# An MLP up-projection as seven block products, its gated product kept in DRAM, and a down-projection that stays in PSUM

## The chip, the core and the metric

The kernel runs on one core of a Trainium2 chip. The metric is device time in microseconds (us). Before the change three runs took 2066.19, 2067.78 and 2071.95 us; the median, 2067.78 us, is the time before.

## What is computed

One transformer block on 1024 tokens of width 1024, all in float32. The change concerns its last part, the residual after the token mixer and the gated MLP with a three-tap convolution over the tokens:

```python
x = x + gt1 * _rmsnorm(y, norm_w[l, 1])                 # y: output of the token mixer, times w_o
h = _rmsnorm(x, norm_w[l, 2]) * (1.0 + sc2) + sh2
hu = _dwconv(h @ w_up, conv_w, FFN_CONV // 2) + conv_b  # w_up: 1024 x 5632
a, b = jnp.split(hu, 2, axis=-1)
y = (jax.nn.silu(a) * b) @ w_down                       # w_down: 2816 x 1024
x = x + gt2 * _rmsnorm(y, norm_w[l, 3])
```

## The kernel before

Every float32 product is made of three float32r products. `split` copies a tile to a rounded high part on ScalarE (L166) and takes the rest as the low part on VectorE or GpSimd (L169). `mm3` (L171) then issues high by high, high by low and low by high into one PSUM group, so a product over K blocks of 128 is 3K matmuls of 128x128 by 128x512. All matmuls have line L128, all transposes L131, which are helpers. Where `T.kept` is set, TensorE follows the program's order; elsewhere a scheduler orders each engine, and each engine works off its own queue in order.

The end of the kernel, from about 1232 us on, goes so:

- `wo_tile(t)` (L1408): for 128 tokens, two PSUM groups `y` of 24 matmuls, with block k = 7 of both halves last. Behind them a chain over ScalarE, VectorE and GpSimd: Square with a running sum (L1423), mean and power -0.5 (L1424 to L1426), scaling (L1429), residual (L1430), store to `x_d`, and the next norm (L1432 to L1435).
- `h2_half` (L1437): 128x128 transposes of four normed token tiles (`x1T`), modulation and split into `h2`, the transposed MLP input, for 512 tokens.
- `up_mm(f)` (L1465): 48 matmuls into a two-bank PSUM tile `hu` for one block f of 128 of the 5632 columns: two token halves, 8 blocks of k, 3 products. The weights `wur` come by DMA 512 KB at a time and are split into `wuh` and `wul`. 44 such blocks make 2112 matmuls.
- `up(f)` (L1504): the convolution as one ScalarE pass (L1508) and two VectorE passes (L1509, L1510). `pair(f)` (L1515): Silu (L1517) of block f, times block 22 + f (L1519), split into `gh` and `gl`.
- `down(c)` (L1542): for two f, 16 groups `yp` of 6 matmuls, each added by VectorE to a running sum `yac` in SBUF (L1551). `last_down` (L1553) takes the last four f, with the final norm and the output behind each token tile. In all 22 x 16 x 3 = 1056 matmuls.

The loop at L1578 to L1584 is four pairs, then in turn `down(c)` and two pairs, then `last_down`. So TensorE alternates between 192 matmuls of up and 96 of down, which have PSUM tiles of their own (2 two-bank tiles for up, 4 banks for down).

Of the kernel before, what the change touches and what calls it, by code (L numbers as in the profile page):

```python
# [32 lines left out]
def prep(inp):  # L33
# [45 lines left out]
    # constants of the shapes  # L79
# [15 lines left out]
class InOrder:  # L95
    """an engine whose instructions, those given here, stay in the order in which they are written"""
# [16 lines left out]
class Tensor:  # L113
    """the tensor engine's queue: kept in the order of the program while `kept`, with a rough clock in us"""
# [19 lines left out]
def build(nc, tc, I, out, dbg=None, stop=None):  # L134
# [87 lines left out]
    with ExitStack() as es:  # L222
# [71 lines left out]
        # token-major columns (beta, alpha, cq, ckv, kr): the first ones along with h  # L294
# [169 lines left out]
    # The tensor engine's queue: chains of dependent steps, each yielding the time until its next one  # L464
    # can start (and what has to be done before), and projections that fill the time between.
# [23 lines left out]
    def filling(convs, gates, w):  # L489
        """projections in turn, the weights of one loaded ahead of the other's use; w: those of the first"""  # L490
# [162 lines left out]
    def tail(h, c):  # L653
        """norm of the sum of both directions"""
# [35 lines left out]
    def head(h):  # L690
        """the norms, the products of k and q, and the rest of the chains of a head"""
# [72 lines left out]
        # token-major k, and v times each direction's beta  # L764
# [62 lines left out]
    def ada_steps():  # L827
        """the other four blocks of the modulation, in pieces to be laid between other work"""
# [35 lines left out]
    def z_steps(ob, h, z):  # L864
        """z of head h, times the normed output of its scans"""
# [102 lines left out]
    def c_norm(t, pl, jpl):  # L968
        """128 tokens of cq and ckv, each divided by its root mean square"""
# [429 lines left out]

    wuE = ExitStack()  # L1400
    wup = pool(wuE, "wup")
    x1E = ExitStack()
    x1p = pool(x1E, "x1p", side="right")
    x1 = [None] * KT
    h2 = [None, None]
    tp = pool(x1E, "so", side="right")

    def wo_tile(t):  # L1408
# [4 lines left out]
        x1[t] = x1p.tile([P, D], F32, tag="x1", name="x1", bufs=6)  # L1413
        pss = [ps_mm.tile([P, 512], F32, tag="mm", name="y") for _ in range(2)]
        for ks in (range(KT - 1), (KT - 1,)):
            for hf in range(2):
                sl = slice(hf * 512, hf * 512 + 512)
                for k in ks:
                    mm3(pss[hf], mg[hf_][0][k][:, c_], mg[hf_][1][k][:, c_], wo[k][0][:, sl], wo[k][1][:, sl], k == 0, k == KT - 1)
        junk = tp.tile([P, D], F32, tag="yj", name="yj")  # L1420
# [16 lines left out]
    def h2_half(hf, pl, tag):  # L1437
        """transposed, modulated and split, one block of columns at a step"""
        h2[hf] = btiles("h2")
        for k in range(KT):  # L1440
            pt = pl.tile([P, 512], F32, tag=tag, name="x1T")
            for j in range(4):
                T.transpose(pt[:, j * P : (j + 1) * P], x1[hf * 4 + j][:, k * P : (k + 1) * P], ident)
            f = tp.tile([P, 512], F32, tag="hf", name="hf2", bufs=2)
            if k % 2 == 0:
                A.activation(f, pt, AF.Identity, bias=sh2[:, k : k + 1], scale=sm2[:, k : k + 1])
            else:
                V.tensor_scalar(f, pt, sm2[:, k : k + 1], sh2[:, k : k + 1], op0=ALU.mult, op1=ALU.add)
            split(h2[hf][0][k], h2[hf][1][k], f)
            yield  # L1450

    for t in range(6):
        wo_tile(t)
    drain(h2_half(0, ps_dn, "dn"))
    wo_tile(6)
    wo_tile(7)
    psE.close()

# [1 line left out]
    psE = ExitStack()  # L1460
    ps_u = pool(psE, "ps_u", 2, space=PSUM)
    ps_y = pool(psE, "ps_y", 4, space=PSUM)
    NF = DFF // P

    def up_mm(f):  # L1465
        wh, wl = w_split(wup, I["w_up"][f], [P, KT, P], "wu", parts=2)
        ps = ps_u.tile([P, S], F32, tag="u", name="hu")

        def mms():
            for hf in range(2):  # L1470
                for k in range(KT):
                    mm3(ps[:, hf * 512 : hf * 512 + 512], wh[:, k, :], wl[:, k, :], h2[hf][0][k], h2[hf][1][k], k == 0, k == KT - 1)
                    yield

        return ps, mms()

    ups_ = {f: up_mm(f) for f in (0, NF)}
    T.kept = True
    (_, ua), (_, ub), tr = *ups_.values(), h2_half(1, ps_y, "y")
    steps = lambda it, n: [next(it) for _ in range(n)]  # L1480
    steps(ua, KT)
    steps(ub, 3)
    steps(tr, 3)
    steps(ub, KT - 3)
    for k in range(KT):
        steps(tr, int(k < KT - 3))
        steps(ua, 1)
        steps(ub, int(k > 2))
    drain(tr)
    T.kept = False  # L1490
    x1E.close()
    kvE.close()
    ffE = ExitStack()
    ff = pool(ffE, "ff")
    yac = [ff.tile([P, D], F32, tag=f"yac{t}", name=f"yac{t}") for t in range(KT)]
    with ExitStack() as es:
        tg = pool(es, "sg", side="right")
        tp = pool(es, "sf", side="right")
        fcw = tp.tile([P, 44, 3], F32, tag="fcw", name="fcw")
        SY.dma_start(fcw, I["f_conv"])  # L1500
        fcb = tp.tile([P, 44], F32, tag="fcb", name="fcb")
        SY.dma_start(fcb, I["f_cb"])
# [12 lines left out]
        def pair(f):  # L1515
            a = up(f)
            A.activation(a, a, AF.Silu)  # L1517
            b = up(NF + f)
            V.tensor_tensor(a, a, b, op=ALU.mult)  # L1519
            gh = tg.tile([P, S], F32R, tag="gh", name="gh", bufs=4)  # L1520
            gl = tg.tile([P, S], F32R, tag="gl", name="gl", bufs=4)
            split(gh, gl, a)
            gs[f] = (gh, gl)

        def load_down(f, hi, lo):
            raw = tg.tile([P, D], F32, tag="wdr", name="wdr", bufs=1)
# [26 lines left out]
        def last_down(fs):  # L1553
# [3 lines left out]
            for t in range(KT):  # L1557
# [12 lines left out]
                for hf in range(2):  # L1570
                    sl = slice(hf * 512, hf * 512 + 512)
                    V.scalar_tensor_tensor(xt[:, sl], yac[t][:, sl], s2[:, 0:1], xt[:, sl], op0=ALU.mult, op1=ALU.add)  # L1572
                    if t == KT - 1:
                        A.dma_start(out[t * P : (t + 1) * P, sl], xt[:, sl])
# [29 lines left out]
```

## Time and profile before

| | |
|---|---|
| median of 3 runs (lowest, highest) | 2067.78 us (2066.19, 2071.95) |
| profiled execution, first to last instruction (span) | 2064.6 us |
| TensorE (PE) busy | 2006.3 us, 97% |
| VectorE (DVE) / ScalarE (ACT) / GpSimd (POOL) busy | 58% / 37% / 16% |
| mean granted TensorE clock | 0.994 |

The profile comes from one execution, for which no time is listed beside its span; the span is 3.2 us under the median and 1.6 us under the lowest run. A busy share is an average over the whole kernel. What a stage can gain or lose is read from that stage, in its windows and in the chain of waits that ended last.

### The profile page before, as it was taken

To read this page: it belongs to the slowest core of one execution; us is meant where nothing else is said; L and a number is where in the kernel's file an instruction comes from. 1 tells how busy PE (TensorE), PEld (TensorE's weight loads), DVE (VectorE), ACT (ScalarE), POOL (GpSimd) and SP (SyncE) were. 2 spreads that over 40 slices of the span, in tenths; PEclk is the share of its full clock that TensorE was granted. 3 is DMA by queue.
4 is the path that set the end of the run, shared out by engine and by line. 5 is a ranking of instruction groups with operands and counts; after the bars stand their busy time and mean duration, and the time that the engine had idled before them with its cause. 6 is when DMAs were issued, how large, how long until landed. Compare 5 with 4: busy or idle time off the path is not lost. (4 is left out here: it accounts for less than half of the span.)

```text
span 2064.6 us, 27272 instructions
## 1 busy us (share of the span) xinstructions
PE 2006.3 (97%) x10846; PEld 1653.6 (80%) x10846; DVE 1204.4 (58%) x2032; ACT 769.1 (37%) x1314; POOL 320.1 (16%) x291
## 2 busy tenths in 40 slices
PE   7999999999999998899999999999999999999998
PEld 5978887888888797778777778878888888888886
DVE  7367867576666568674677654553435444445437
ACT  6464543353353222353545432443222222222222
POOL 4321131141041110233000031110100001000101
PEclk9999999999999999999999999999999999999999
DMA  8321121131021175454101163221111112111113
GB/s 291 112 72 62 43 72 57 47 113 62 32 99 66 44 262 193 149 158 151 53 11 32 41 200 106 73 82 41 52 52 51 42 42 62 41 51 41 51 47 137
DMA packets 68178, 175.09 MB, mean 85 GB/s; under 512 B 10257, under 2 KB 17745, under 8 KB 68050
## 3 DMA queue, kind: packets, MB, share of 16 engines
q1 hardware_dynamic: 54658, 143.13, 21.9%
q10 hardware_dynamic: 11088, 21.83, 2.8%
q0 software_dynamic: 2304, 8.39, 1.0%
q8 instruction: 85, 1.39, 0.3%
q14 instruction: 43, 0.35, 0.1%
HBM read 143.07 MB, written 30.24 MB: 84 GB/s over the span
## 5 line engine op out<-in xcount | busy, mean ns | idle before, releaser
L128 PE MATMUL hu<-h,wuh 128*128 128x512 f32 x1408 | 434.2, 390 | 1.6 <-DVE cv L1510 1.6
L128 PEld LDWEIGHTS hu<-h,wuh 128*128 128x128 f32 x1408 | 263.8, 188 | 56.6 <-ACT cv L1508 2.0
L128 PE MATMUL pj<-hhi,wth 128*128 128x512 f32 x704 | 294.1, 418 | 8.1 <-ACT vN L906 6.6
L128 PE MATMUL pj<-hhi,wtl 128*128 128x512 f32 x704 | 277.7, 394 | 0.0
L128 PE MATMUL pj<-hlo,wth 128*128 128x512 f32 x704 | 276.2, 392 | 0.0
L128 PE MATMUL hu<-h,wul 128*128 128x512 f32 x704 | 274.0, 389 | 0.0
L128 PEld LDWEIGHTS pj<-hhi,wth 128*128 128x128 f32 x704 | 133.8, 190 | 29.1 <-ACT vN L906 7.0
L128 PEld LDWEIGHTS pj<-hhi,wtl 128*128 128x128 f32 x704 | 132.9, 189 | 28.7
L169 DVE TENSOR_TENSOR wul<-wur,wuh 128x512 fp32r<-128x512 f32 x44 | 30.4, 692 | 214.9 <-ACT wuh L166 214.8
L128 PEld LDWEIGHTS hu<-h,wul 128*128 128x128 f32 x704 | 132.2, 188 | 27.5
L169 POOL TENSOR_TENSOR wul<-wur,wuh 128x512 fp32r<-128x512 f32 x44 | 57.8, 1313 | 612.6 <-ACT wuh L166 535.8
L128 PEld LDWEIGHTS pj<-hlo,wth 128*128 128x128 f32 x704 | 133.9, 190 | 20.2
L128 PE MATMUL yp<-wdh,gl 128*128 128x512 f32 x336 | 132.7, 395 | 0.0
L128 PE MATMUL yp<-wdh,gh 128*128 128x512 f32 x336 | 132.7, 395 | 0.0
L128 PE MATMUL yp<-wdl,gh 128*128 128x512 f32 x336 | 132.6, 395 | 0.0
L169 POOL TENSOR_TENSOR wtl<-wtr,wth 128x512 fp32r<-128x512 f32 x44 | 62.2, 1414 | 412.5 <-ACT wth L166 327.5
L166 ACT CAST wuh<-wur 128x512 fp32r<-128x512 f32 x88 | 53.9, 614 | 188.4 <-PE hu L128 188.4
L1551 DVE TENSOR_TENSOR yac<-yac,yp 128x512 f32<-128x512 f32 x128 | 87.0, 685 | 53.6 <-PE yp L128 53.1
L128 PE MATMUL y<-wo,mg 128*128 128x512 f32 x384 | 89.1, 391 | 0.7 <-ACT mg L166 0.7
L128 PEld LDWEIGHTS y<-wo,mg 128*128 128x128 f32 x384 | 71.6, 188 | 16.1 <-ACT mg L166 1.1
L166 ACT CAST wth<-wtr 128x512 fp32r<-128x512 f32 x88 | 53.3, 617 | 81.9 <-PE pj L128 56.2
L166 ACT CAST wdh<-wdr 128x1024 fp32r<-128x1024 f32 x21 | 22.0, 1049 | 159.9 <-PE yp L128 110.6
(442 smaller groups left out, 4081.5 us busy)
## 6 DMA issues: line engine op xcount, KB each, us to landing
wtr<-w_t SPq DMA_DIRECT2D x44, 512.0 KB, 3.5
wur<-w_up SPq DMA_DIRECT2D x44, 512.0 KB, 3.6
adaw<-w_adaT SPq DMA_DIRECT2D x64, 256.0 KB, 4.0
gt_d<-gate ACTq DMA_DIRECT2D x48, 256.0 KB, 2.0
g<-gt_d SPq DMA_DIRECT2D x24, 512.0 KB, 3.6
wdr<-w_dn SPq DMA_DIRECT2D x22, 512.0 KB, 3.5
ada_w<-w_adaT SPq DMA_DIRECT2D x16, 512.0 KB, 6.0
wbr<-w_br SPq DMA_DIRECT2D x24, 256.0 KB, 3.8
```

The source lines that it names most:

```text
L128: self.queue(self.nc.tensor.matmul(out, w, x, **kw), x, 4 if x.dtype == F32 else 1)
L166: ins = A.copy(hi, src)
L169: (eng or V).tensor_tensor(lo, src, r32(hi), op=ALU.subtract)
L1551: V.tensor_tensor(yac[t][:, sl], yac[t][:, sl], ps, op=ALU.add)
```

## The change

The up-projection now treats a pair p = (block p, block 22 + p) of weight columns, two halves of the 1024 input features and two halves of the tokens as 2x2 blocks, and makes seven products of 12 matmuls instead of eight: A11 B11, A12 B21, P3 T3, P2 T2, P1 T1, A22 T4 and P4 B22. P1 to P4 are sums of weight blocks, made for each pair (L1494, L1496 on VectorE, L1495, L1497 on GpSimd) and split; T1 to T4 are sums of input blocks, made once (`t_ops`). The products add up in place in two two-bank PSUM tiles per pair, `uA` and `uB`, two pairs in turn, which take all eight banks. Between products come a copy of A11 B11 into the other half of `uA` (L1542, ScalarE), a copy `m7` of P3 T3 (L1600, ScalarE) and two additions from `uA` plus `m7` into `uB` (L1605 and L1610, VectorE). The gated product goes to DRAM (`g_d`, L1629, issued by ScalarE's queue). When all 22 pairs are done, the down-projection runs for four token tiles at a time with its sums in the same four PSUM tiles; each block of w_down and of `g_d` is loaded and split once for each of the two groups. The additions to `yac` are gone, and the final norm reads PSUM. Numbers of lines in this section and of `uA`, `uB` are those of the kernel after.

Ahead of it, `wo_tile` makes its two halves one after the other, each with k = 7 last; `x1` has 2 buffers instead of 6; the transposes are done token tile by token tile (`h2_tile`) into float32 tiles `F`. The big tiles are eight of 4 x 512 columns. Cut to its core:

```diff
 def wo_tile(t):
-        for ks in (range(KT - 1), (KT - 1,)):
-            for hf in range(2):
-                for k in ks: mm3(pss[hf], ...)
+        for hf in range(2):
+            for k in range(KT): mm3(pss[hf], ...)
+    def up_load(p):
+        for f in (p, NF + p):
+            r.append(wup.tile([P, KT, P], F32, tag="wur", name="wur", bufs=3))
+            SY.dma_start(r[-1], I["w_up"][f])
+        o = [wup.tile([P, KT, P], F32R, tag="wu1", name=f"wu1{m}", bufs=4) for m in "hl"]
+        split(o[0], o[1], r[0])
+    def up_sums(p, w):
+        V.tensor_tensor(p3, a11, a21, op=ALU.add)
+        G.tensor_tensor(p1, a21, a22, op=ALU.add)
+        V.tensor_tensor(p2, a11, p1, op=ALU.add)
+        G.tensor_tensor(p4, a12, p2, op=ALU.add)
+        for nm, src, shape, eng in (("32", s32, [P, KT, P], V), ("14", s14, [P, KT, P], G), ("22", a22, [P, 4, P], V)):
+            o[nm] = [pl.tile(shape, F32R, tag="wu" + nm, name=f"wu{nm}{m}", bufs=4 if nm != "14" else 2) for m in "hl"]
+            split(o[nm][0], o[nm][1], src, eng)
+    T.kept = True
+    for t in range(KT):
+        wo_tile(t)
+        if t > 0:
+            h2_tile(t - 1, [ps_dn.tile([P, 512], F32, tag="dn", name="x1T") for _ in range(2)])
...
+    uA = [ps_u.tile([P, S], F32, tag=f"uA{n}", name="uA") for n in range(2)]
+    uB = [ps_u.tile([P, S], F32, tag=f"uB{n}", name="uB") for n in range(2)]
+    def first(p):
+        a, b = uA[p % 2][:, half[1]], uA[p % 2][:, half[0]]
+        prod(a, W[p]["A11"], X["B11"], True)
+        A.copy(b, a)
+    def second(p):
+        prod(uA[p % 2][:, half[0]], W[p]["A12"], X["B21"], False)
+    first(0); second(0); first(1)
+    h2_tile(KT - 1, [uB[0][:, half[0]], uB[0][:, half[1]]])
+    second(1)
+    t_ops(slice(0, 384), sums, 384)
+    t_ops(slice(384, 512), sums, P)
+    def third(p):
+        e = uB[p % 2][:, half[0]]
+        prod(e, W[p]["P3"], X["T3"], True)
+        A.copy(m7s[p], e)
+    def fourth(p):
+        a, e = uA[p % 2][:, half[1]], uB[p % 2][:, half[0]]
+        prod(a, W[p]["P2"], X["T2"], False)
+        V.tensor_tensor(e, a, m7s[p], op=ALU.add)
+    def fifth(p):
+        a, d = uA[p % 2][:, half[1]], uB[p % 2][:, half[1]]
+        prod(a, W[p]["P1"], X["T1"], False)
+        V.tensor_tensor(d, a, m7s.pop(p), op=ALU.add)
+    def last_two(p):
+        prod(uB[p % 2][:, half[0]], W[p]["A22"], X["T4"], False)
+        prod(uA[p % 2][:, half[1]], W[p]["P4"], X["B22"], False)
+    def gated(p):
+        a = conv(p, uA[p % 2])
+        A.activation(a, a, AF.Silu)
+        b = conv(NF + p, uB[p % 2])
+        V.tensor_tensor(a, a, b, op=ALU.mult)
+        A.dma_start(g_d[p], a)
+    third(0); fourth(0); third(1); fifth(0); last_two(0); gated(0)
+    fourth(1); fifth(1); last_two(1); gated(1)
+    for p in range(2, NF):
+        first(p); third(p); fourth(p); second(p); fifth(p); last_two(p); gated(p); prep(p + 2)
+    def down_mm(gr, f, t, hf):
+        mm3(ys[t][:, half[hf]], g[0][:, tk], g[1][:, tk], wd[0][:, half[hf]], wd[1][:, half[hf]], f == 0, f == NF - 1)
+    def finish(gr, t, hf, c):
+        A.activation(o[:, half[hf]], ys[t][:, half[hf]], AF.Square, accum_out=s2[:, hf : hf + 1])
...
```

The order of instructions of the kernel after, at three places, with the semaphores that an instruction waits for. First TensorE in pair 2: the end of P2 T2 (`fourth`), the first rows of A12 B21 (`second`), the end of P1 T1 and the start of A22 T4.

```order
L128 MATMUL uA<-T2l,wu32h 128x512
L128 MATMUL uA<-T2h,wu32l 128x512
L128 MATMUL uA<-B21h,wu1h 128x512 [waits DVE_49]
L128 MATMUL uA<-B21l,wu1h 128x512
...
L128 MATMUL uA<-T1l,wu14h 128x512
L128 MATMUL uA<-T1h,wu14l 128x512
L128 MATMUL uB<-T4h,wu22h 128x512 [waits DVE_49]
L128 MATMUL uB<-T4l,wu22h 128x512
```

Two products of each pair now begin with a wait for VectorE: `second`, which writes the first half of `uA` (the VectorE count that it waits for is that of the addition L1605, which reads the second half of the same tile), and A22 T4 (its count is that of L1610, which writes the second half of the same `uB`). Each stands directly behind the product whose result that addition reads. Before, the matmuls of `hu` waited only for a free tile.

Then VectorE through one pair, from the convolution of the pair before (`uA_13090`) to the addition L1610 of this one (`uB_13093`):

```order
L1620 SCALAR_TENSOR_TENSOR cv_13560<-uA_13090,fcw_13228,cv_13560 128x1023 [waits DMAHW0_49,Activation_49]
L1620 SCALAR_TENSOR_TENSOR cv_13565<-uB_13092,fcw_13228,cv_13565 128x1023 [waits Activation_49]
L1621 SCALAR_TENSOR_TENSOR cv_13560<-uA_13090,fcw_13228,cv_13560 128x1023 [waits DVE_49]
L1621 SCALAR_TENSOR_TENSOR cv_13565<-uB_13092,fcw_13228,cv_13565 128x1023 [waits DVE_49]
L1496 TENSOR_TENSOR s32_13579<-wur_13571,s14_13580 128x512 [waits Pool_49]
L1628 TENSOR_TENSOR cv_13560<-cv_13560,cv_13565 128x1024 [waits DVE_49,Activation_49]
L1605 TENSOR_TENSOR uB_13093<-uA_13091,m7_13622 128x512 [waits PE_49]
L169 TENSOR_TENSOR wu32l_13586<-s32_13579,wu32h_13585 128x1024 [waits Activation_49]
L1494 TENSOR_TENSOR s32_13705<-wur_13697,wur_13699 128x512 [waits DMAHW2_49,DMAHW4_49,DVE_49,Pool_49]
L169 TENSOR_TENSOR wu1l_13702<-wur_13697,wu1h_13701 128x1024 [waits PE_49,Activation_49]
L1610 TENSOR_TENSOR uB_13093<-uA_13091,m7_13622 128x512 [waits PE_49]
```

The two additions that TensorE waits for stand behind other work of VectorE: L1605 behind the convolution and the gating product of the pair before, L1610 behind the weight work of the pairs ahead, one of which (L1494) waits for a DMA.

Last, VectorE between the last token tile's modulation and the first pair's weights (`T..` are the input sums, `wu32` the weights P3 and P2 of pair 0, whose product is `third(0)`):

```order
L1459 TENSOR_SCALAR F1_12386<-uB_13092,sm2_7566,sh2_7567 128x128 x3
L1557 TENSOR_TENSOR t3_13181<-F1_12386 128x1536 [waits DVE_49]
L1559 TENSOR_TENSOR t1_13182<-F0_12385,F1_12386 128x1536
L169 TENSOR_TENSOR T3l_13172<-t3_13181,T3h_13171 128x4x384 [waits Activation_49]
...
L169 TENSOR_TENSOR T4l_13178<-t4_13202,T4h_13177 128x4x128 [waits Activation_49]
L1494 TENSOR_TENSOR s32_13233<-wur_12899,wur_12901 128x512 [waits DMAHW0_49,DMASW6_49]
L1496 TENSOR_TENSOR s32_13233<-wur_12899,s14_13234 128x512 [waits Pool_49]
...
L169 TENSOR_TENSOR wu32l_13240<-s32_13233,wu32h_13239 128x1024 [waits Activation_49]
```

All sums and splits of the input, and the weight sums, stand in one VectorE chain behind the last token tile and ahead of `third(0)`; before, `h2` was split block by block between matmuls of the first two up-blocks.

## Rows read from the trace of the kernel before

**Rows 1.** The page, section 1: busy us, share of the span, instructions

```profile
PE 2006.3 (97%) x10846; PEld 1653.6 (80%) x10846; DVE 1204.4 (58%) x2032; ACT 769.1 (37%) x1314; POOL 320.1 (16%) x291
```

**Rows 2.** Windows; columns: PE, PEld, DVE, ACT, POOL busy us, granted clock, DMA

```profile
1400.00:1500.00 100.00, 100.00 (x438) 81.90 (x437) 38.61 (x40) 31.88 (x43) 7.76 (x6) 1.00 0.15 48
```

**Rows 3.** The chain that ended last; start us, us, engine, tile, line

```profile
1417.59 22.39 PE yp L128 x96
1439.98 43.53 PE hu L128 x192
```

**Rows 4.** First matmuls of `y`, timeline; start us, us, engine, operation [idle <-releaser]

```profile
1232.12 4.24 PE L128 MATMUL y<-wo,mg 128*128 128x512 f32 x18
1237.08 61.77 PE L128 MATMUL y<-wo,mg 128*128 128x512 f32 x270 [0.72 <-ACT mg L166]
...
1240.90 1.29 DVE L169 TENSOR_TENSOR mg<-g,mg 128x512 fp32r<-128x512 f32 x2
```

**Rows 5.** Tile `yac`; duration ns minimum/median/maximum, first and last start

```profile
L1551 DVE TENSOR_TENSOR yac<-yac,yp x128: 673/686/690, 1484.9 to 1967.4; 128x512 f32<-128x512 f32 x128
...
L1565 ACT ACTIVATE yj<-yac x16: 618/632/633, 2019.8 to 2057.4; 128x512 f32<-128x512 f32 x16
L1565 ACT ACTIVATION_READ_ACCUMULATOR yj<-yac x16: 185/187/188, 2020.4 to 2057.9; 128x1 f32 x16
```

**Rows 6.** Timeline, a group of `yp` that ends and the addition behind it

```profile
1626.17 0.39 PE L128 MATMUL yp<-wdh,gl 128*128 128x512 f32 x1
...
1626.60 0.69 DVE L1551 TENSOR_TENSOR yac<-yac,yp 128x512 f32<-128x512 f32 x1 [0.71 <-PE yp L128]
```

**Rows 7.** Timeline, TensorE behind a VectorE pass that frees `hu`

```profile
1350.63 1.28 DVE L1510 SCALAR_TENSOR_TENSOR cv<-hu,fcw,cv 128x1023 f32<-128x1023 f32 x1
...
1352.06 0.70 PE L128 MATMUL hu<-h,wuh 128*128 128x512 f32 x2 [1.60 <-DVE cv L1510]
```

**Rows 8.** Tile `hu`, the convolution's ScalarE pass

```profile
L1508 ACT ACTIVATE cv<-hu,fcb,fcw x44: 1200/1203/1207, 1348.1 to 2011.0; 128x1024 f32<-128x1024 f32 x44
```

**Rows 9.** Timelines of ScalarE and VectorE, Silu and gating product

```profile
1353.65 1.06 ACT L1517 ACTIVATE cv<-cv 128x1024 f32<-128x1024 f32 x1
...
1620.98 1.22 DVE L1519 TENSOR_TENSOR cv<-cv 128x1024 f32<-128x1024 f32 x1
```

**Rows 10.** Tile `wur`, splits of 512 columns, and the load

```profile
L166 ACT CAST wuh<-wur x88: 602/616/627, 1241.3 to 1990.9; 128x512 fp32r<-128x512 f32 x88
...
L169 DVE TENSOR_TENSOR wul<-wur,wuh x44: 681/692/694, 1242.3 to 1990.0; 128x512 fp32r<-128x512 f32 x44
L169 POOL TENSOR_TENSOR wul<-wur,wuh x44: 1285/1292/1922, 1242.5 to 1991.7; 128x512 fp32r<-128x512 f32 x44
...
DMA to landing us min/median/max: 3.4/3.6/5.5
```

**Rows 11.** Tile `wdr`, the cast of 1024 columns

```profile
L166 ACT CAST wdh<-wdr x21: 1047/1049/1051, 1343.0 to 1973.0; 128x1024 fp32r<-128x1024 f32 x21
```

**Rows 12.** Timeline, behind the last matmul of token tile 7's `y`

```profile
1324.89 0.62 PE L128 MATMUL hu<-h,wuh 128*128 128x512 f32 x2
...
1329.67 1.06 ACT L1432 ACTIVATE yj<-xt 128x1024 f32<-128x1024 f32 x1 [3.90 <-DVE xt L1430]
...
1331.69 0.75 DVE L1435 TENSOR_SCALAR x<-xt,s 128x1024 f32<-128x1024 f32 x1 [0.69 <-POOL s L1434]
```

**Rows 13.** Windows, TensorE at a long and a short wait, columns as above

```profile
790.00:796.00 6.00, 3.90 (x9) 3.16 (x10) 4.28 (x14) 1.43 (x4) 1.47 (x1) 0.51 0.84 280
...
854.00:858.00 4.00, 2.16 (x12) 1.91 (x13) 3.13 (x7) 1.04 (x1) 1.11 (x1) 1.00 0.16 29
```

**Rows 14.** Timeline of TensorE at the long wait

```profile
792.10 0.80 PE L128 MATMUL pj<-hhi,wth 128*128 128x512 f32 x1 [6.55 <-ACT vN L906]
```

**Rows 15.** Timeline, a GpSimd subtraction beside one of VectorE

```profile
1242.28 0.69 DVE L169 TENSOR_TENSOR wul<-wur,wuh 128x512 fp32r<-128x512 f32 x1
1242.53 1.59 POOL L169 TENSOR_TENSOR wul<-wur,wuh 128x512 fp32r<-128x512 f32 x1 [6.15 <-ACT wuh L166]
```

More of the change, by code (lines that the diff above doesn't have):

```diff
@@ L1435, in wo_tile, with h2_tile @@
         V.tensor_scalar(x1[t], xt, s2[:, 2:3], None, op0=ALU.mult)
[L1437 to L1441, printed above, removed]
+    def h2_tile(t, pts):
+        hf_, c_ = t // 4, slice((t % 4) * P, (t % 4) * P + P)
+        for n, pt in enumerate(pts):
             for j in range(4):
[L1443 to L1450, printed above, removed]
@@ L1457, in build @@
     psE.close()
     psE = ExitStack()
[L1461 to L1490, printed above, removed]
+    ps_u = pool(psE, "ps_u", space=PSUM)
+    uA = [ps_u.tile([P, S], F32, tag=f"uA{n}", name="uA") for n in range(2)]
@@ new lines, in build, with t_ops @@
+    second(0)
+    first(1)
+    hxE = ExitStack()
+    def t_ops(cols, sums, n):
+        f11, f21, f12, f22 = F[0][:, 0:4, cols], F[0][:, 4:8, cols], F[1][:, 0:4, cols], F[1][:, 4:8, cols]
+        t3, t1, t2, t4 = (sums.tile([P, 4, n], F32, tag=f"t{k}", name=f"t{k}") for k in (3, 1, 2, 4))
+        V.tensor_tensor(t3, f22, f12, op=ALU.subtract)
+        x_split("T3", cols, t3)
+        V.tensor_tensor(t1, f11, f12, op=ALU.subtract)
+        V.scalar_tensor_tensor(t2, t1, -1.0, f22, op0=ALU.mult, op1=ALU.subtract)
+        x_split("T2", cols, t2)
+        x_split("T1", cols, t1, G)
+        V.scalar_tensor_tensor(t4, t2, -1.0, f21, op0=ALU.mult, op1=ALU.subtract)
+        x_split("T4", cols, t4)
+        x_split("B22", cols, f22, G)
@@ L1585, in build @@
-    ffE.close()
+    hx = pool(hxE, "hx", side="right")
+    tsE = ExitStack()
+    sums = pool(tsE, "sums", side="right")
+    for nm in ("T3", "T2"):
+        x_op(nm)
+    for nm in ("T1", "T4", "B22"):
+        x_op(nm, hx, nm)
+    t_ops(slice(0, 384), sums, 384)
+    t_ops(slice(384, 512), sums, P)
+    tsE.close()
+    fE.close()
+    epE = ExitStack()
+    ep = pool(epE, "ep")
+    ffE = ExitStack()
+    wus = pool(ffE, "wus", side="right")
+    tg = pool(ffE, "sg")
+    fcw = tg.tile([P, 44, 3], F32, tag="fcw", name="fcw")
@@ new lines, in gated, with prep @@
+    def gated(p):
[4 more added lines that the diff above has]
+        A.dma_start(g_d[p], a)
+    def prep(p):
+        if p < NF:
+            if p not in W:
+                W[p] = up_load(p)
+            up_sums(p, W[p])
+    for p in range(2):
+        prep(p)
+    third(0)
+    fourth(0)
+    third(1)
+    fifth(0)
+    last_two(0)
+    gated(0)
+    prep(2)
+    fourth(1)
+    fifth(1)
@@ new lines, in build, with down_step @@
+    last_two(1)
+    gated(1)
+    prep(3)
+    for p in range(2, NF):
+        first(p)
+        third(p)
+        fourth(p)
+        second(p)
+        fifth(p)
+        last_two(p)
+        gated(p)
+        prep(p + 2)
+    ffE.close()
+    hxE.close()
+    dnE = ExitStack()
+    dw = pool(dnE, "dw", side="right")
+    ys = [uA[0], uB[0], uA[1], uB[1]]
+    steps = {}
+    def down_step(gr, f):
+        raw = wup.tile([P, D], F32, tag="wur", name="wdr", bufs=3)
+        SY.dma_start(raw, I["w_dn"][f])
+        graw = dw.tile([P, 512], F32, tag="gr", name="gr", bufs=4)
+        SY.dma_start(graw, g_d[f][:, gr * 512 : gr * 512 + 512])
+        pl, n = (ep, 1) if (gr, f) == (0, 0) else (dw, 6)
+        wd = [pl.tile([P, D], F32R, tag=f"wd{m}", name=f"wd{m}", bufs=n) for m in "hl"]
+        gg_ = [pl.tile([P, 512], F32R, tag=f"g{m}", name=f"g{m}", bufs=n) for m in "hl"]
+        split(gg_[0], gg_[1], graw)
+        split(wd[0], wd[1], raw, G if f % 3 == 2 else V)
+        steps[gr, f] = wd, gg_
@@ new lines, in build, with get @@
+    LAST = NF - 4
+    order = [(gr, f) for gr in range(2) for f in range(NF)]
+    ahead = iter(order)
+    def get(n):
+        for _ in range(n):
+            if (o := next(ahead, None)) is not None:
+                down_step(*o)
+    get(5)
+    for gr in range(2):
+        f0 = 0
+        if gr == 0:
+            for ts in ((0, 1), (2, 3)):
+                for f in range(3):
+                    for t in ts:
+                        for hf in range(2):
+                            down_mm(gr, f, t, hf)
+            get(3)
+            f0 = 3
+        for f in range(f0, LAST):
+            for t in range(4):
+                for hf in range(2):
+                    down_mm(gr, f, t, hf)
+            get(1)
+        for t in range(4):
+            c = {}
+            for hf in range(2):
+                for f in range(LAST, NF):
+                    down_mm(gr, f, t, hf)
+                finish(gr, t, hf, c)
+        get(4 if gr == 0 else 0)
@@ L1586, in build @@
+    T.kept = False
+    dnE.close()
+    epE.close()
     wuE.close()
```

193 lines of the change are left out of this document (99 added, 94 removed).

## The prediction

> **What bounds the kernel now.** I read the page first: TensorE is busy for 97% of the span [rows 1]. That is an average, so I went on to the windows of the last 700 us. In each of them TensorE is busy without a break at granted clock 1.00, that is at 2.4 GHz, while VectorE is busy for 38.6% [rows 2], the first of six windows with TensorE at 100%. The chain of waits says the same in time order: from 1352 to 2052 us it is matmuls only, 192 of up (43.53 us) and 96 of down (22.39 us) in turn, nine times over [rows 3]. So the end of the kernel is a queue of matmuls with nothing in between: a matmul removed is worth its spacing, and each wait that the change puts into that queue costs its full length. TensorE's own waits there are small (the longest is 1.60 us [rows 7]).
>
> **Matmuls removed.** The spacing isn't one number: 0.2267 us in up (groups of 24 matmuls into one bank), 0.2288 in `y` (61.77 us for 270 [rows 4], groups of 21 and 3, 12 on the mean) and 0.2332 in down (groups of 6). These three fit 0.2246 us a matmul plus 0.052 us at each change of bank (an estimate from the three rows: 0.2268, 0.2289, 0.2333). Up goes from 2112 matmuls in 88 groups (478.9 us) to 22 x 84 = 1848 in 154 (423.1): **-55.8 us**. Down keeps its 1056, but changes the bank every 3 matmuls, and every 12 for the last four f: 304 groups in place of 160, **+7.5** (0 if the fit means something else, 9 with groups of 3 throughout). The Trainium skill ("TensorE: Matmul & The Clock Gate", section "Back-to-back issue gap") gives 131 ns as the sustained spacing at 512 columns, by which the 264 matmuls would be an estimated 34.6 us and the result 21 us worse; the rows show no stretch nearer to that than 224 ns, so I go by the rows.
>
> **Weight, convolution and sum work** on ScalarE, VectorE and GpSimd costs nothing by itself while TensorE has matmuls to run. The same holds for what goes away (the 128 additions to `yac`, 0.69 us each [rows 5], were under cover of matmuls). What counts is the places where TensorE now waits for these engines.
>
> **Steady pairs (20 of them).** TensorE's list shows two waits for VectorE with no cover: each addition needs the product just ended, and the next product needs the addition, since one tile holds both halves. The least price comes from three rows: 0.20 us from the end of a group's last slot (1626.40) to the addition behind it [rows 6], 0.69 for an addition of 512 columns that reads PSUM [rows 5], and 0.15 from the end of a VectorE pass (1351.91) to the matmul that it releases (1352.06) [rows 7]. That is 1.04 us twice a pair, the floor of 2.1 us. Whether VectorE comes in time I walked through, with t = 0 at the start of a pair: the convolution of the pair before begins on ScalarE behind a cast of 1.05 us [rows 11] and ends its first pass (1.20 us [rows 8]) at 2.4; four VectorE passes of 1.28 [rows 7], 1.20 apart, then a weight sum of 0.69 [rows 10], bring VectorE to 7.9, and the gating product of 1.22 [rows 9], free to start as Silu (1.06 [rows 9]) ended at 7.2, to 9.0. P2 T2 ends at 8.16. The addition is thus late: 8.94 to 9.63, and `second` starts at 9.78 in place of 8.16, a wait of 1.62 us. For the other addition: a load is issued when GpSimd has finished P4 (9.3), lands 3.6 us later [rows 10] at 12.9, and L1494 and a low part of 1.22 end at 15.0, before P1 T1 does (15.22); so this wait is the least one, 1.04. Together 2.66 us a pair, times 20: **+53**. Bounds: the floor, 42, and 3.5 us a pair, 70, if loads land late.
>
> **Into the pairs (pairs 0 and 1).** Let 0 be the end of token tile 7's `y` (1324.89 [rows 12]). Until the input sums exist TensorE has the last transposes and four products, 13.1 us in all. The copy of the first product stands on ScalarE behind tile 7's second Square, which ends at 5.8 [rows 12], and a cast of 1536 columns (1.48 us, an estimate along the line of 0.62 and 1.05 us for 512 and 1024 [rows 10, 11]), so `second(0)` waits 4.3 us; the normed tile 7 itself comes at 7.6 [rows 12]. With 1.3 us more at the transposes, TensorE is out of work at 18.7 and `F` complete at 16.9. Then VectorE's list ahead of `third(0)`: seven operations of 1536 columns (1.75 each, an estimate along 0.69 and 1.22 [rows 9, 10]), ten of 512 and the low part `wu32l` of 1024, in all 12.3 + 6.9 + 1.2 = 20.4 us. Since only the third matmul needs that last part, TensorE idles from 18.7 to about 36.3: 17.6 us. Behind it P1 T1 of pair 1 waits some 5.9 us, because the split weights of P1 and P4 have one pair of buffers and the next split can't start before pair 0's last product has ended; A22 T4 of pair 0 waits 1.4. A long wait also lowers the clock: behind 6.55 us of idleness [rows 14] nine matmuls took 3.9 us at granted 0.51, that is at 1.2 GHz, in place of 2.0 [rows 13], so 1.9 us for each of two. Sum 4.3 + 1.3 + 17.6 + 7.3 + 3.8: **+34** (26 to 42, by how the three engines interleave).
>
> **From up to down.** All tiles of PSUM hold pair 21, and ScalarE's list has the last convolution, Silu, the issue of the last store (behind the gating product), three casts of w_down and the cast of g before the first down matmul: 0.2 + 1.2 + 4 x 1.23 + 1.22, then 3 x 1.05 + 0.62 [rows 7 to 11], which is 11.3 us; the low part of g some 1 us later, and 1.9 for the clock: **+14** (11 to 17).
>
> **Smaller terms.** In `wo_tile(0)` the first half now needs `mg` of k = 7 after 21 matmuls instead of 42: TensorE would reach it at 1237.8, its low part, the first of the two operations shown, ends at 1241.6 [rows 4]: **+3.5** (0 to 5.5). The final sums: each second half of a `ys` tile waits for the Square of the first (0.63 + 0.19 [rows 5] + about 0.2) in its eight last turns: **+8** (6 to 9). The wait of 1.60 us of before [rows 7] goes: **-1.6**; a shorter chain behind the last matmul (one addition and one multiplication of 0.69 fewer [rows 5]): **-1.3**.
>
> **Sum.** -55.8 + 7.5 + 53 + 34 + 14 + 3.5 + 8 - 1.6 - 1.3 = +61.3. The span goes from 2064.6 to about 2125.9; the profiled span lies 3.2 us under the median of the runs, so the time is **2129 us**, 3% slower. All low bounds together give +26 (2094), all high ones, with up at 3 us more, +97 (2165).
>
> **Rivals.**
> - *The pair waits don't bite* (the other side). If the two counts that `second` and A22 T4 wait for were reached earlier than the additions end, or the additions fell under cover, the steady term would be near 0; with the transition at 26, the boundary at 11 and no price for bank changes the sum is -55.8 + 26 + 11 + 3.5 + 6 - 2.9, about -12: 2055 us. It decides where the loss of a pair is under some 0.6 us. For it: VectorE is under half busy. Against it: the order of the additions, directly between the two products. Chance 0.09, of which 0.03 ends within 0.3% (what a measurement of this kernel can tell from no change).
> - *The clock falls in the pairs.* If each of 20 pairs had one stretch at 1.2 GHz, at 1.9 us, that is +38: 2167 us. Against it: in the window at 854 TensorE was idle for 1.84 us, more than any wait of a pair, and the clock stayed at 1.00 [rows 13]. Chance 0.06.
> - *GpSimd is held up by VectorE.* A GpSimd subtraction took 1.59 us where VectorE subtracted in SBUF beside it, 1.29 otherwise [rows 15, 10]. In a pair, P4 runs beside the gating product; up to 1.1 us later it delays the load and the second addition by 0.4 to 1 us: +8 to +20, 2137 to 2149 us. Chance 0.15. The Trainium skill ("SBUF — State Buffer", section "SBUF: two separate sides") says that a VectorE operation with two SBUF inputs and a GpSimd operation lock each other out of a shared port for a whole instruction; [rows 15] agree in direction, with 0.3 us.
> - *Loads land late.* At 5.5 us, the longest landing [rows 10], the second addition ends 1.5 us later: +30, 2159 us. Chance 0.10.
>
> **How the numbers follow.** My forecast has 0.60. With the last two rivals it lies within 2085 to 2165, which leaves out the first two, 0.15, and takes in the bounds. Faster 0.06, within 0.3% 0.03, slower 0.91.
>
> **What would show it.** Right: in the windows of the pairs TensorE busy for about 88% at clock 1.00, its waits headed by additions L1605 and L1610 in some 44 waits of 1.0 to 1.6 us; a hole of 15 to 20 us behind the transposes, with VectorE on L1557 to L1563 and L169; one of some 12 us before the first down matmul. Wrong: waits at L1605 or L1610 of under 0.5 us, or a pair that takes under 20 us (21.9 by the sum), or a spacing of 0.227 us in down.

## The result and the profile after

The change makes the kernel slower: 2125.72 us, median of four runs (2124.79 to 2129.94), against 2068.61 us for the kernel before in the same series (2066.19 to 2071.95). The ratio is 1.0285, with a 95% interval of 1.0266 to 1.0303. The forecast was 2129 us.

Page of the kernel after, section 1 (busy us, share, instructions) and the clock in 40 slices:

```profile
PE 1969.2 (93%) x10584; PEld 1609.5 (76%) x10584; DVE 1243.9 (59%) x2055; ACT 856.1 (40%) x1418; POOL 440.7 (21%) x335
...
PEclk9999999999999999999999999799999999989999
```

TensorE went from 97% [rows 1] to 93%. It does 262 matmuls less (264 fewer in the products, and two that start tiles of pairs 0 and 1) and is busy for 37 us less, in a span that is 58.7 us longer: the time went into idleness. The two dips of the clock, at slices 26 and 36, mark the two places where it stood longest.

Windows of the kernel after, columns as in [rows 2]: pairs 0 and 1, the other 20 pairs, the boundary between up and down, and down.

```profile
1326.90:1414.90 88.00, 49.62 (x188) 37.92 (x187) 52.32 (x55) 30.99 (x42) 28.80 (x15) 0.79 0.15 49
1414.90:1847.70 432.80, 392.85 (x1681) 312.03 (x1679) 235.91 (x233) 156.74 (x176) 114.11 (x58) 1.00 0.22 73
1847.70:1861.50 13.80, 0.12 (x1) 0.00 (x0) 7.84 (x7) 6.86 (x8) 1.44 (x1) 0.66 0.24 91
...
1861.50:2115.70 254.20, 245.78 (x1056) 199.27 (x1056) 87.03 (x114) 74.68 (x114) 38.47 (x21) 0.98 0.49 156
```

Before, TensorE had no break in such windows [rows 2]. Now it stands for 38 of 88 us in the first, for 40 of 433 in the second and for all of the third. VectorE is at 55% in the steady pairs: no engine there is full, so it is the order that costs time.

The waits of TensorE (tile, line <- releaser: us in total, times, longest us):

```profile
PE uB L128 <- ACT wu32h L166: 23.6, 1, 23.6
PE uA L128 <- DVE uB L1605: 22.6, 20, 1.2
PE uB L128 <- DVE uB L1610: 19.6, 22, 2.3
PE uA L128 <- ACT gh L166: 13.7, 1, 13.7
PE uA L128 <- ACT cv L1626: 5.6, 1, 5.6
...
PE uA L128 <- ACT uA L1542: 3.9, 1, 3.9
...
PE uA L128 <- ACT yo L1696: 3.1, 4, 0.8
```

Two kinds are seen. The additions L1605 and L1610 cost a little in every pair, 42 times. The first product with sums of both sides (`wu32h`) and the first down product (`gh`) cost much, once each; such a place, where TensorE has nothing to do, is called a hole below.

The chain that ended last shows the period of the steady pairs, and the down-projection (start us, us, engine, tile):

```profile
1430.86 3.01 PE uB L128 x12
...
1445.90 5.75 PE uA L128 x24
...
1452.42 3.01 PE uB L128 x12
...
1885.50 1.36 PE uA L128 x6
```

A22 T4 starts every 21.56 to 21.60 us in 17 of the 20 pairs; the last three take 23.1, 21.6 and 21.2. 84 matmuls at 0.2267 us are 19.04, so a pair loses 2.54 us. In down, 6 matmuls take 1.36 us, which is 0.2267 each: the spacing of up, not that of down before (22.39 us for 96 [rows 3]).

One steady wait in the timeline (start us, us, engine, operation [idle <-releaser]):

```profile
1616.64 1.22 DVE L1628 TENSOR_TENSOR cv<-cv 128x1024 f32<-128x1024 f32 x1
...
1617.78 0.69 DVE L1605 TENSOR_TENSOR uB<-uA,m 128x512 f32<-128x512 f32 x1
...
1618.53 0.50 PE L128 MATMUL uA<-B21h,wu1h 128*128 128x512 f32 x1 [1.15 <-DVE uB L1605]
```

The addition stands right behind the gating product of the pair before (L1628), and `second` starts 0.06 us after the addition ends.

### The profile page after: what moved, and what is told of

The parts are those of the page before. It is cut to its first block, busy times and chain, and to the rows that moved or that the text cites. A ratio compares the mean times of both kernels' runs of the same rounds, so it can differ in the third digit from the quotient of the medians.

```text
span 2123.3 us, 27228 instructions
## 1 busy us (share of the span) xinstructions
PE 1969.2 (93%) x10584; PEld 1609.5 (76%) x10584; DVE 1243.9 (59%) x2055; ACT 856.1 (40%) x1418; POOL 440.7 (21%) x335
## 3 DMA queue, kind: packets, MB, share of 16 engines
q8 instruction: 83, 1.36, 0.3%
## 5 line engine op out<-in xcount | busy, mean ns | idle before, releaser
L169 POOL TENSOR_TENSOR wu14l<-s,wu14h 128x1024 fp32r<-128x1024 f32 x22 | 52.8, 2399 | 273.0 <-ACT wu14h L166 273.0
L169 DVE TENSOR_TENSOR gl<-gr,gh 128x512 fp32r<-128x512 f32 x44 | 30.7, 706 | 117.1 <-ACT gh L166 117.1
L128 PE MATMUL uA<-wdh,gh 128*128 128x512 f32 x176 | 69.9, 397 | 16.8 <-ACT gh L166 13.7
L579 ACT CAST tU<-pu 128x512 f16<-128x512 f32 x80 | 44.2, 587 | 94.1 <-PE pu L128 93.5
L128 PE MATMUL uB<-wdh,gh 128*128 128x512 f32 x176 | 69.6, 395 | 3.7 <-ACT yo L1696 3.1
L169 POOL TENSOR_TENSOR wdl<-wdr,wdh 128x1024 fp32r<-128x1024 f32 x14 | 36.1, 2576 | 176.2 <-ACT wdh L166 176.2
L573 DVE TENSOR_TENSOR pm<-pp,msk 128x512 f16<-128x512 f32 x96 | 63.4, 686 | 15.7 <-PE pp L128 15.0
L584 DVE CAST tT<-pq 128x512 f16<-128x512 f32 x96 | 62.8, 684 | 15.3 <-PE pq L128 15.0
L128 PE MATMUL uA<-wdh,gl 128*128 128x512 f32 x176 | 69.2, 393 | 1.5 <-DVE gl L169 1.5
L128 PE MATMUL uA<-wdl,gh 128*128 128x512 f32 x176 | 69.1, 393 | 0.0
```

The costliest lines, as they stand in the source:

```text
L128: self.queue(self.nc.tensor.matmul(out, w, x, **kw), x, 4 if x.dtype == F32 else 1)
L169: (eng or V).tensor_tensor(lo, src, r32(hi), op=ALU.subtract)
L573: V.tensor_tensor(pm, v4(pp), b4(msk[:, l, 1 - d, :]), op=ALU.mult)
L579: A.copy(nU, v4(pu))
L584: V.tensor_copy(nT, v4(pq))
```

## The experiments

Single runs start the first `y` matmul anywhere between 1228.7 and 1236.2 us, though nothing ahead of it differs. So beside each time I give the stretch from the first `y` matmul to the end of the span: 832.5 us before, 894.0 after. Kernels with a ratio were run four times, the others once.

### Tiles of one bank, and the finer convolution alone

If the steady waits come from one tile's holding both halves, so that `second` must wait for an addition that only reads the other half, then tiles of one bank remove them. Those tiles need the convolution in halves, which the second kernel does alone.

```diff
-    uA = [ps_u.tile([P, S], F32, tag=f"uA{n}", name="uA") for n in range(2)]
+    uA = [[ps_u.tile([P, 512], F32, tag=f"uA{n}{h}", name=f"uA{h}") for h in range(2)] for n in range(2)]
...
-        A.activation(o, ps, AF.Identity, bias=fcb[:, f : f + 1], scale=fcw[:, f, 1:2])
+        for h, q in zip(half, (p0, p1)):
+            A.activation(o[:, h], q, AF.Identity, bias=fcb[:, f : f + 1], scale=fcw[:, f, 1:2])
```

> Each half of uA, uB and of the down sums is a PSUM tile of its own; products, sums and their order stay. Theory (two tile-wide waits a pair without cover): the waits for L1605 and L1610, 2.5 us a pair, go, since the next product now covers each addition; a pair takes 19.1 us instead of 21.6, the eight waits for the Square in down (7 us) and the 1.6 us at the last transposes go as well: about 2067 us. Rival (VectorE, GpSimd and the loads set the pace of a pair): the waits turn up at other instructions, a pair stays above 21 us, and the time above 2105 us.

> Control for the first run: the two-bank tiles stay, but the convolution is done in two halves of 512 columns as there (4 ScalarE and 8 VectorE passes a pair instead of 2 and 4). If the gain of the first run comes from the tiles and not from finer passes, nothing moves: 2126 us within 3, a pair 21.6 us. Rival: finer passes let VectorE reach the addition L1605 earlier, a pair takes some 0.3 us less, 2119 us.

The one-bank tiles took 2054.83 us (stretch 823.8), ratio to the kernel before 0.9955 (0.9939 to 0.9972): slightly faster than before, and better than I expected. Its window over the steady pairs, and its chain:

```profile
1407.00:1790.00 383.00, 381.46 (x1682) 315.07 (x1680) 268.14 (x317) 171.75 (x217) 116.99 (x58) 1.00 0.25 82
```

```profile
1412.68 8.16 PE uA L128 x36
1420.84 2.72 PE uB L128 x12
...
1431.72 8.16 PE uA L128 x36
```

The period is 19.04 us in 17 of the 20 pairs and 19.2 to 19.3 in the others: next to nothing is lost. The stretch is 70.2 us shorter: 52 in the steady pairs, 9 to 10 where the final Squares had held up the second half of a tile, 7 in pairs 0 and 1 (the waits of 1.6 us and those for L1610 are gone, that of 5.6 us is down to 3.5) and 1.5 at the boundary (12.2 for 13.7).

The finer convolution alone took 2172.92 us (stretch 937.8, 43.8 more than the change), where I had expected no difference. So the gain belongs to the tiles. Eight passes of 0.7 us keep VectorE longer than four of 1.28 did, it reaches L1605 later, and TensorE waits 1.89 us instead of 1.15. Timeline and windows of that wait:

```profile
1619.70 0.50 PE L128 MATMUL uA<-B21h,wu1h 128*128 128x512 f32 x1 [1.89 <-DVE uB L1605]
...
1620.64 0.63 PE L128 MATMUL uA<-B21h,wu1h 128*128 128x512 f32 x1
1621.07 0.63 PE L128 MATMUL uA<-B21l,wu1h 128*128 128x512 f32 x1
```

```profile
1621.00:1624.00 3.00, 3.00 (x9) 2.31 (x8) 0.94 (x2) 0.00 (x0) 0.00 (x0) 0.54 0.63 199
1624.00:1628.00 4.00, 3.21 (x15) 2.33 (x14) 1.92 (x2) 1.05 (x1) 0.00 (x0) 1.00 0.00 0
```

Behind it the granted clock is 0.54, near the lower level of 1.2 GHz, and eight matmuls come 0.43 us apart, which costs some 1.6 us a pair. The prediction's rival "the clock falls in the pairs" did not occur in the change, where the five microseconds behind a wait of 1.15 us had 1.00. But the length of a wait alone does not decide: here 1.89 us lowered the clock in 18 pairs one after another and left it at 1.00 in the first, and in the change itself the longest wait of a steady pair, 2.26 us, left it at 1.00:

```profile
1799.22 0.50 PE L128 MATMUL uB<-T4h,wu22h 128*128 128x512 f32 x1 [2.26 <-DVE uB L1610]
```

```profile
1799.00:1804.00 5.00, 4.78 (x21) 3.93 (x22) 0.86 (x2) 0.62 (x1) 0.00 (x0) 1.00 0.22 84
```

### GpSimd and VectorE in front of the first sums

In the change VectorE runs slow there. Timeline of both engines:

```profile
1349.01 1.75 DVE L1559 TENSOR_TENSOR t<-F,F 128x1536 f32<-128x1536 f32 x1
1350.67 2.82 DVE L169 TENSOR_TENSOR T3l<-t,T3h 128x1536 fp32r<-128x1536 f32 x1
1353.42 4.97 DVE L1560 SCALAR_TENSOR_TENSOR t<-t,F 128x1536 f32<-128x1536 f32 x1
```

```profile
1352.34 4.43 POOL L169 TENSOR_TENSOR T1l<-t,T1h 128x1536 fp32r<-128x1536 f32 x1 [0.46 <-ACT T1h L166]
```

L1560 starts at 1353.42 beside a GpSimd subtraction that runs to 1356.77, ends 1.6 us behind it, and takes 4.97 us for a size that takes 1.75 alone: it did nearly all its work when the other was done. The experiment gives that subtraction to VectorE.

```diff
-        x_split("T1", cols, t1, G)
+        x_split("T1", cols, t1)
```

> The low part of T1 (two operations) moves from GpSimd to VectorE. Theory (VectorE's operations on two SBUF operands stand still while GpSimd works): the pass L1560 of 1536 columns takes 1.75 us instead of 4.97, VectorE has 2.4 us more to do and loses some 5 us of delays, third(0) starts about 3 us earlier: 2123 us. Rival (L1560 is slow for another reason): it stays near 5 us and third(0) starts 2 us later: 2128 us.

Measured 2128.41 us (stretch 894.2, no gain in all). L1560 came down to 1.75 us, as the theory says. But VectorE has two operations more, and the small subtraction left on GpSimd now loses in turn:

```profile
1351.75 8.73 POOL L169 TENSOR_TENSOR B22l<-F,B22h 128x512 fp32r<-128x512 f32 x1 [10.78 <-ACT B22h L166]
...
1360.44 2.77 POOL L1495 TENSOR_TENSOR s<-wur 128x512 f32<-128x512 f32 x1
```

8.73 us instead of 1.29 [rows 10], and beside the next GpSimd sum two VectorE passes took 2.8 instead of 1.75. The mechanism is shown; the remedy moved most of it. Counted from the first `y` matmul, `third(0)` starts 1.0 us earlier than in the change and pair 2 1.8 us earlier. The stretch hides this, because one late pair took 23.2 us instead of 21.6: behind a wait of 2.25 us the granted clock fell to 0.52.

### The order of the sums over k in `y`

```diff
-        for hf in range(2):
-            sl = slice(hf * 512, hf * 512 + 512)
-            for k in range(KT):
+        for ks in (range(KT - 1), (KT - 1,)):
+            for hf in range(2):
```

> The output projection again takes k = 7 of both halves last, as in the kernel before. Theory: the wait of 2.6 us in the first token tile shrinks to about 0.7 and its stretch at 1.2 GHz (some 2 us) goes: 2122 us. Rival: the stretch comes from the activity before and not from this wait, only 1.9 us go: 2124 us.

Measured 2124.71 us, stretch 889.9: the wait of 2.6 us and the half clock behind it are gone, 4.1 us less, close to what I expected of it (the `y` stage itself is 4.7 us shorter, and the same late pair lost 1.5 us to the clock). The time itself shows little of that, since this run reached `y` 3.7 us later.

### Up to down: memory, then the order

In the change, the first casts of the down stage wait for memory that holds the last gating product until it is stored, and three of them stand ahead of the cast of g on ScalarE:

```profile
1855.31 0.33 ACTq L1629 DMA_DIRECT2D g_d<-cv  x1
1858.00 2.94 ACT L166 CAST wdh<-wdr 128x1024 fp32r<-128x1024 f32 x3 [4.09 <-DMA g_d<-cv]
1860.84 2.17 ACT L166 CAST gh<-gr 128x512 fp32r<-128x512 f32 x4
```

ScalarE stood 4.09 us, until the store had landed, then cast, and the first down matmul came at 1861.51. Two kernels on top of the one-bank tiles change this: the first takes other tiles into that memory and issues the last store from GpSimd's queue (two things at once, which the run does not tell apart), the second moves the first three down steps and their memory ahead of the last pair's gating.

```diff
+    early = {"x": dw.tile([P, D], F32, tag="xr", name="x1r", bufs=3), "o": dw.tile([P, D], F32, tag="yo", name="yo", bufs=3)}
...
-        A.dma_start(g_d[p], a)
+        (G if p == NF - 1 else A).dma_start(g_d[p], a)
```

```diff
-    get(5)
+    get(3)
+    gated(NF - 1)
+    ffE.close()
+    get(5 - 3)
```

> On top of one-bank tiles: the down tiles gr and wd no longer lie where the last pair's cv lay, and the last store is issued by GpSimd. Theory (the hole ahead of down is first the store's landing, since the first weight cast reuses that memory, then ScalarE's order): the casts start some 4 us earlier, behind Silu, the hole shrinks from 12.2 to about 8.5 us: 2051 us. Rival (only ScalarE's order and the convolution count): the hole stays above 11 us: 2055 us.

> On top of the memory change the first three steps of down are written ahead of the last pair's gate (five buffers instead of six), so the cast of g for f = 0 stands ahead of the last Silu on ScalarE. Theory: the first down matmul starts about 2 us after the last of up instead of 12.2, without a stretch at 1.2 GHz: 2041 us. Rival (down needs the tiles of the last pair anyway): the hole moves to the matmuls of token tiles 2 and 3 and more than 5 us of it stays: 2047 us.

The first took 2056.44 us, stretch 818.4, that is 5.4 less than with the one-bank tiles alone; the hole fell from 12.2 to 8.1 us (8.5 expected). The second took 2044.89 us, stretch 813.8, another 4.6 less. Its wait is 3.3 us, where I had expected about 2, and the stretch at 1.2 GHz that was to go stayed (granted 0.50 from 1792.5 to 1797.5):

```profile
PE uA L128 <- ACT gh L166: 3.3, 1, 3.3
```

### Into the pairs: sums earlier

The sums of 384 tokens need nothing of the last token tile. This kernel, with one-bank tiles, does them ahead of that tile's transposes, which takes memory on the other side.

```diff
     first(0)
-    second(0)
     first(1)
+    kvE.close()
...
+    t_ops(slice(0, 384), sums, 384)
+    second(0)
     h2_tile(KT - 1, [uB[0][0], uB[0][1]])
```

> On top of one-bank tiles: three quarters of the input sums (token tiles 4 to 6) are made before the last token tile is normed, in memory freed by the output weights, and first(1) stands ahead of second(0). Theory (VectorE's chain behind the last tile sets the hole ahead of third(0)): seven operations of 1536 columns leave the chain, the hole of 23.5 us shrinks to about 11, the wait for the copy (3.9 us) goes: 2038 us. Rival (GpSimd and VectorE hold each other up wherever these operations stand): VectorE's operations of 1536 columns still take up to 5 us, the hole stays above 16 us: 2046 us.

Measured 2049.68 us, stretch 816.7: 7.1 less, where I had expected some 17. The hole fell from 23.5 to 12.8 us, but the copy of the first product stayed late, twice now (6.6 us in all), and the norm of the last tile met GpSimd:

```profile
1337.60 3.93 DVE L1444 TENSOR_SCALAR x<-xt,s 128x1024 f32<-128x1024 f32 x1 [0.46 <-POOL s L1443]
1341.45 5.01 DVE L1566 SCALAR_TENSOR_TENSOR t<-t,F 128x1536 f32<-128x1536 f32 x1
```

```profile
1337.54 3.44 POOL L169 TENSOR_TENSOR B22l<-F,B22h 128x1536 fp32r<-128x1536 f32 x1
1340.95 3.90 POOL L169 TENSOR_TENSOR T1l<-t,T1h 128x1536 fp32r<-128x1536 f32 x1
```

L1444 took 3.93 us; it takes 0.75 otherwise [rows 12].

### All together

> One-bank tiles, earlier input sums, and down's first steps ahead of the last gate. If the gains are at separate places they add: 2054.8 - 14 - 17 = 2024 us. If the holes only hand on to one another, above 2035 us.

Earlier sums and earlier down loads together: 2040.0 us, ratio 0.9875 (0.9856 to 0.9895), stretch 808.5. The two gains over the one-bank tiles, 10.0 and 7.1 us, would give 806.7, so they nearly add; my 2024 took the expected gain of the earlier sums, and fell short with it. Two more edits go at what was left: all low parts of the sums on VectorE, and the first product of pairs 0 and 1 made twice by TensorE instead of copied.

```diff
-        x_split("T1", cols, t1, G)
+        x_split("T1", cols, t1)
...
-        x_split("B22", cols, f22, G)
+        x_split("B22", cols, f22)
```

```diff
+            prod(b, W[p]["A11"], X["B11"], True)
         prod(a, W[p]["A11"], X["B11"], True)
-        A.copy(b, a)
+        if p >= 2:
+            A.copy(b, a)
```

> On top of all three changes: the low parts of T1 and B22 move from GpSimd to VectorE (4.9 us more of VectorE's work ahead of third(0)). Theory (an operation of VectorE with SBUF operands stands still while GpSimd works, and the other way round): the norm's scaling of the last token tile (L1444) takes 0.75 us again and not 3.9, no operation of 1536 columns takes over 2 us, some 9 us of standing still go, third(0) starts some 4 us earlier: 2036 us. Rival (these operations are slow for their place, not for GpSimd): they stay slow, third(0) starts 5 us later: 2045 us.

> On top of that, pairs 0 and 1 compute A11 B11 into both halves of uA (12 matmuls more each) instead of a copy by ScalarE. Theory (the copy stands behind three casts of 1536 columns): two waits of together 6.7 us and a stretch at 1.2 GHz of 2 us go for 5.4 us of matmuls, 3 us less than the run before: 2033 us. Rival (TensorE then waits the same time for the last tile's transposes): no change, 2036 us.

With the low parts on VectorE: 2037.53 us, stretch 803.8, 4.7 less; with no GpSimd subtraction left beside them, L1444 is back at 0.75 us, and `third(0)` starts 4.5 us earlier. With the doubled first product: 2035.55 us (2034.51 to 2036.34), ratio 0.9852 (0.9836 to 0.9869), stretch 801.5. This is the fastest version, 1.5% under the kernel before and 4.2% under the change as it stood. What still waits in it:

```profile
PE uB L128 <- ACT wu32h L166: 13.8, 1, 13.8
PE uA L128 <- DVE uB L1607: 3.5, 1, 3.5
PE uA L128 <- ACT gh L166: 3.3, 1, 3.3
```

### Why down is faster per matmul

The prediction's spacing of down rested on three rows of before. One candidate for the slower 0.2332 us there was VectorE reading PSUM beside it. This is the kernel before without the additions to `yac`:

```diff
-                    else:
-                        V.tensor_tensor(yac[t][:, sl], yac[t][:, sl], ps, op=ALU.add)
```

> The kernel before, without the 128 additions to yac (these partial sums are left out of the result; the copies for the first two f and the last four f stay). It asks why matmuls of down came every 0.2333 us there. If VectorE's reading of PSUM right behind each group slows TensorE, the 96 matmuls of a down block take 21.8 us instead of 22.4: about 5 us less in all, 2060 us. If the groups of 6 or the tiles of g themselves do, they stay at 22.4: 2065 us.

Measured 2064.54 us, stretch 832.7, and the groups of down as long as before:

```profile
1415.76 22.39 PE yp L128 x96
```

So those additions are not the cause. (This run leaves part of the sum out of the result.)

## Why the prediction was right

The sum was +61.3 us and the span grew by 58.7. By terms:

| term | predicted | measured |
|---|---|---|
| matmuls removed in up | -55.8 | -60.0 (22 x 19.04 for 478.9) |
| spacing of down | +7.5 | -6.8 (1056 x 0.2267 for 246.2) |
| 20 steady pairs | +53 | +52.0 (432.8 less 20 x 19.04) |
| pairs 0 and 1 | +34 | +47.7 (88.0 less 2 x 19.04 and 2.2 of transposes) |
| up to down | +14 | +18.6 |
| `wo_tile`, second half earlier | +3.5 | +4.7 |
| final Squares | +8 | +9.9 |
| `y` begins earlier, by chance | none | -2.9 |
| old wait, tail | -2.9 | -3.2 |
| sum | +61.3 | +60.0 |

The last 1.3 us between 60.0 and 58.7 I did not trace; some transposes moved from one stage to another, which no term counts.

**Steady pairs: right, by the walk.** I took 2.66 us a pair and it was 2.54 on 17 of 20, 2.60 on the mean. The shape was a little off: 1.62 and 1.04 us were expected, about 1.4 and 1.1 came. The one-bank tiles show the cause by taking the waits away whole, so "the pair waits don't bite" falls. A load was late once, in the pair of 23.1 us: the first one of w_down, issued when the sum P4 (L1497) had freed its buffer; its cast stood ahead of a weight cast of the pair.

**Down: wrong, and in sign.** The step that failed is the fit of a price of 0.052 us for each change of bank. Down now changes bank every 3 matmuls for most of its length and runs at 0.2267 us, which the prediction had named as a sign of being wrong. The step was worth 14.3 us, and 4.2 us of up's term come from the same fit. The trace of before already spoke against it. The 0.2288 us of `y` was an average over a slow start behind a wait and a steady stretch, and the 224 ns that I named is no row but the fit's own figure. Timeline of the steady stretch, with the same groups of 21 and 3:

```profile
1244.74 45.49 PE L128 MATMUL y<-wo,mg 128*128 128x512 f32 x200
```

These are 199 spacings of 0.2266 us and the last matmul's 0.39. And in the old down-projection all six matmuls of a group came 0.229 to 0.238 us apart, not only the one at the change of bank; the first two of a group:

```profile
1420.22 0.40 PE L128 MATMUL yp<-wdh,gh 128*128 128x512 f32 x1
1420.46 0.39 PE L128 MATMUL yp<-wdl,gh 128*128 128x512 f32 x1
```

The matmul's own price was rightly taken from rows. The Trainium skill ("TensorE: Matmul & The Clock Gate", section "Back-to-back issue gap") gives 131 ns, by which the 264 matmuls would be worth an estimated 34.6 us; the measured 60.0 contradicts it. What made down slower before stays open; the additions to `yac` are excluded.

**Into the pairs: right places, too small.** The copy wait (3.9 for 4.3) and the transposes (1.6 for 1.3) came as walked. P1 T1 of pair 1 waited 5.6 us for 5.9, but by luck. Timelines of GpSimd, VectorE and TensorE:

```profile
1395.76 2.38 POOL L169 TENSOR_TENSOR wu14l<-s,wu14h 128x1024 fp32r<-128x1024 f32 x1 [14.64 <-ACT wu14h L166]
```

```profile
1402.19 0.69 DVE L1605 TENSOR_TENSOR uB<-uA,m 128x512 f32<-128x512 f32 x1
```

```profile
1403.03 0.77 PE L128 MATMUL uA<-T1h,wu14h 128*128 128x512 f32 x1 [5.57 <-ACT cv L1626]
```

The split weights, which I had taken for the cause, were ready at 1398.14. What it waited for is the addition L1605, which reads the half of `uA` that this product writes and stands on VectorE behind the convolution of pair 0. (The view names the Silu, L1626, which ends at nearly the same moment; in the runs with one-bank tiles and with the finer convolution it names L1605 for this wait.)

Two things failed. The hole was 23.6 us for 17.6, because I added VectorE's operations at their lone durations: L1560 alone was 3.2 us longer, the low part `T3l` 1.1, and two passes of 512 columns 1.1 each (1.78 and 1.75 for 0.68), all beside GpSimd. I had that rival, but placed it in the steady pairs, where P4 did slow to 2.18 us and, but for the one late load, nothing waited for it. And three stretches ran at half clock where I had counted two, 33 matmuls at 0.43 us instead of 0.23:

```profile
1334.70:1339.70 5.00, 5.00 (x12) 3.98 (x13) 0.00 (x0) 0.00 (x0) 3.03 (x1) 0.50 0.00 0
...
1372.30:1377.30 5.00, 4.33 (x9) 3.01 (x10) 2.31 (x2) 1.59 (x2) 3.60 (x3) 0.50 0.65 203
...
1403.00:1408.00 5.00, 4.97 (x12) 3.80 (x12) 3.54 (x3) 0.85 (x1) 0.63 (x1) 0.50 0.64 202
```

A wait of 3.94 us stood ahead of the first. The hole and the clock make 8.8 of the 13.7 us that were missing; three waits of 0.6 to 0.8 us are part of the rest, which I did not trace further.

**Up to down: 4.6 us too small.** 13.9 us passed before the first matmul, where 11.3 was predicted. ScalarE's list was right up to the issue of the store at 1855.31 (7.7 us behind the last product, 7.5 predicted). I left out that w_down's cast needs memory which the store still held, and the cast began 2.4 us later than the issue was over. Behind the first matmul, `gl` and half clock cost 4.7 us, where I had allowed 2.7.

**Final Squares: right place, a little too small** (9.9 us, where I had allowed 6 to 9). Timeline:

```profile
2112.58 0.50 PE L128 MATMUL uB<-wdh,gh 128*128 128x512 f32 x1 [0.78 <-ACT yo L1696]
```

Eight of these, 1.1 us each from slot to slot and with the slower matmuls behind, and one of 0.6 us for L1703.

So the total was met by a right main term and by errors that cancel, which is luck: 18.5 us too much on the spacing of up and down (4.2 and 14.3), 18.3 too little on pairs 0 and 1 and the boundary.

## What to carry to other kernels

Fewer matmuls pay only if the additions between the products stay off TensorE's path: in place in one tile they cost 2.54 us of each 2.7 us product saved, and splitting the tile by bank gave all of it back. Put the first steps of a new stage (its memory, its loads, its sums) ahead of the last work of the old one. And in a walk along VectorE's list, give each operation that runs beside a GpSimd tensor operation the price of both.

## What the runs showed of the hardware

- GpSimd and VectorE hold each other up for much of an operation, either way round: VectorE went from 1.75 to 4.97 and 5.01 us and from 0.75 to 3.93, GpSimd from 1.29 to 8.73. L1560 ended 1.62 us behind the GpSimd operation beside it, about its whole time alone. [rows 15] had shown only 0.3 us. The Trainium skill ("SBUF — State Buffer", section "SBUF: two separate sides") calls it an exclusive lock on a shared port under which the other "fully blocks"; these durations agree.
- In a dense stream, waits of 1.15 us left the granted clock at 1.00. Waits of 1.89 us lowered it to about half for some 3 us in 18 pairs and left it at 1.00 in one; 2.26 us left it at 1.00 in the change, and 2.25 us at the same place in the run with T1 on VectorE lowered it to 0.52. Before, the 1.84 us of idleness of [rows 13], part of one wait of 2.51 us, had left it at 1.00. So one row with the clock at 1.00 is no evidence that a wait of that size is free, as I took it.
- The spacing of matmuls isn't a matter of bank changes: 0.2267 us with one every 3. Behind each wait of 0.8 us the matmul next to it came 0.34 us before its follower, the next five (in the pairs) to nine (at the final Squares) at about 0.233 us and the rest at 0.227; why is open.
